# Loading the parameters of a mixer and making its tables during the feed-forward before it, in a four-layer decoder trunk

## The chip, the cores and the metric

The kernel runs on one core of one Trainium2 chip. The metric is the device time of one execution in microseconds (us); the time of a kernel is the median of several runs. Engines: PE is the matrix engine, with a queue of its own for loading weights (PEld), DVE the vector engine, ACT the scalar engine, POOL the general one, and SP the engine whose queue issues the DMAs.

## What is computed

Four layers over 256 tokens of width 1024, in float32. Each layer has three sub-layers, and each of those is applied as

```python
x = layer_norm(DN_ALPHA * x + f(x), g, b)
```

The first sub-layer is the mixer: a Conformer convolution in layers 0 and 3, a Mamba-2 mixer in layer 1, differential attention in layer 2. The second is attention to 256 memory tokens, the third a SwiGLU feed-forward. Of the mixers, what bears on the change is where small parameters enter:

```python
# Conformer: w_dw is 31 taps x 1024 channels
h = a * sigmoid(gate)                      # a, gate = split(x @ w_in + b_in)
h = causal_depthwise_conv(h, w_dw, b_dw)
# Mamba-2: 32 heads; w_conv 4 x 4096, b_conv 4096, norm_g 2048; dt_bias, a_log, d_skip 32 numbers each
dt = softplus(dt + dt_bias); a = -exp(a_log)
y = y + d_skip * xs
# differential attention: lam from exp(sum(lq1 * lk1)) - exp(sum(lq2 * lk2)); subln_g 128 numbers
```

## The kernel before

The 256 tokens are two tiles of 128. x stays on the chip; its transpose is kept as a sum of two reduced-precision parts, XTh and XTl, and every product of float32 matrices is three matmuls (`mm3`, L176 to L178: high x high, low x high, high x low). All weights are streamed, each once, in 537 blocks of 128 x 1024 numbers (512 KB). `_Weights` reads a plan of the whole order of blocks, which a first pass of the same program has recorded, and fetches three blocks ahead. For a block, SP issues a DMA into one of four buffers raw (L125), ACT casts it to wh (L132), and DVE subtracts in two halves to make the rest wl (L135); wh and wl have rings of seven buffers. The raw buffers also serve for other loads of up to 128 x 1024 numbers: the DFT constants (dft), the taps, the rows of the Mamba-2 parameters, some biases. A load that takes a raw buffer has to wait until the block that was in it has been cast and subtracted, and the blocks after it do with one buffer less until its own reader is done.

Each engine carries out its instructions in the order of the program as a scheduler has placed them, and a DMA on SP waits there, with all that is behind it, until its buffer is free. After each sub-layer `post_norm` adds and normalises x tile by tile (L311 the sum, L219 the statistics, L318 and L323 the norm, on DVE) and transposes it again on PE (L196; the splits are L183 on ACT and L185 on DVE). Between these, PE works on kv units, the projections of the memory for the next attention (psi from MTh, MTl).

The mixers begin with their small parameters, in the mixer's own code:

- `conv` (layers 0 and 3) multiplies by w_in in four pieces, `gated(0)` to `gated(3)`, and does the depthwise convolution through a real DFT over 160 points. After `gated(0)` it loads dft into a raw buffer (L465) and splits it, loads taps into another (L475) and the bias yre (L480), makes the spectra H of the taps by four float32 matmuls of 31 rows (L483; the chip records two for each), which ACT copies out of PSUM (L484), and, in layer 0, loads and transposes the memory (L364). Then come `gated(1)` and the rest.
- `ssd` (layer 1) loads sd_rows and sd_rows2 into two raw buffers (L712, L714, L715), transposes them on PE, loads sd_dcol by two DMAs of 64 x 16 single numbers (L727), sd_dtb (L732) and sd_ea (L734), and ACT takes the exponential of sd_ea (L735). Its first matmuls make dt.
- `diff` (layer 2) loads da_lv by four DMAs (L1044) and da_sg by one (L1056), multiplies and sums da_lv on DVE (L1047, L1050), takes an exponential on ACT (L1051), scales da_sg (L1057) and makes a mask.

`ff` works through 11 chunks of 256 hidden columns. All tile pools of a stage are opened with the default rule for their memory's reuse.

Of the kernel before, what the change touches and what calls it, by code (L numbers as in the profile page):

```python
# [9 lines left out]
F32 = mybir.dt.float32  # L10
# [7 lines left out]
P = 128  # L18
# [52 lines left out]
class _Trace:  # L71
    """Stands for the engines and the tiles while the order of the weight blocks is recorded."""
# [16 lines left out]

class _Weights:  # L90
    """Streams [128, nk, n] blocks of the weights and splits each into two float32r parts,
    whose sum is the float32 block."""
# [51 lines left out]
class _Trunk:  # L144
# [28 lines left out]
    def mm3(self, out, ah, al, bh, bl, start, stop):  # L173
        """Adds the float32 product of two split operands (a stationary, b moving)."""
# [5 lines left out]
    def split(self, src, dh, dl, scale=1.0):  # L180
        """dh + dl = scale * src, dh and dl in float32r."""
# [23 lines left out]
    def rstd(self, var, eps, cols, scale=1.0):  # L205
        """(scale * var + eps) ** -0.5"""
# [36 lines left out]
    def gemm_a(self, name, i, segs, done, which="o"):  # L243
        """x @ w[:, segs] for 512 columns, natural: tile 0 through all of them, then tile 1."""
# [15 lines left out]
    def out_mm(self, acc, t, h, w, first, last):  # L260
        """Adds rows h (128 of them, transposed) times their block of weights, tokens of tile t."""
# [16 lines left out]
    def out_tail(self, acc, name, i, ks, hs, ln, nxt=True, first=False):  # L278
        """The last blocks: tile 0 through all of them, then tile 1, each with its LayerNorm."""
# [15 lines left out]
    def new_xt(self, wanted=True):  # L295
        """The transposed activations for the next stage, if there is one."""
# [106 lines left out]
    def conv(self, i, j):  # L403
        """The depthwise convolution goes through a real DFT of 160 points over the tokens: tile t's
        128 outputs need the 30 tokens before them and its own."""
# [631 lines left out]
    def diff(self, i, j):  # L1037
# [3 lines left out]
        with tc.tile_pool(name="da", bufs=1) as pool, tc.tile_pool(name="dw", bufs=2) as wk:  # L1041
            lv = pool.tile([P, 4, 64], F32, name="da_lv")
            for q, name in enumerate(("da_lq1", "da_lk1", "da_lq2", "da_lk2")):
                nc.sync.dma_start(out=lv[:, q, :], in_=ins[name][j].partition_broadcast(P))  # L1044
# [275 lines left out]
```

## Time and profile before

| | us |
|---|---|
| runs (3), median and extremes | 1792.8 (1787.34 to 1801.01) |
| span of the profiled execution, first to last instruction | 1784.0 |
| PE busy | 1726.5 (97%) |
| DVE busy | 1241.6 (70%) |
| ACT busy | 850.0 (48%) |
| mean granted clock of PE | 0.987 |

The profiled execution's time outside its span is not recorded; the median of the runs is 8.8 us above the span, the fastest run 3.3 us. A row of the windows gives, for a stretch of time, the busy time of each engine with the number of its instructions, the clock granted to PE as a share of the full one, the busy share of the DMA engines and the rate. A row of a timeline gives start, duration, engine, line and operation, and in brackets how long the engine was idle before it and what ended that; SPq is SP issuing a DMA.

### The profile page before, as it was taken

The numbers are of one execution on the slowest core, as the hardware profiler recorded it, in microseconds if no ns is written. First come the engines' busy times: TensorE is split into PE (matmuls) and PEld (weight loads), VectorE is DVE, ScalarE is ACT, GpSimd is POOL, SyncE is SP. The second block draws the span as 40 slices with busy tenths as digits, with TensorE's granted clock in tenths as the row PEclk, the third lists the DMA queues.
The fourth block names the chain that finished last, engine by engine and source line by source line (L and its number), as shares of the span: only waits on it lengthen the run. The fifth ranks groups of instructions, "written<-read, shape, count | busy, mean of one in ns | idle before, by whom it ended". The sixth has DMA issues, their size and how long they took to land.

```text
span 1784.0 us, 29260 instructions
## 1 busy us (share of the span) xinstructions
PE 1726.5 (97%) x11356; PEld 1558.5 (87%) x11356; DVE 1241.6 (70%) x2296; ACT 850.0 (48%) x1258; POOL 56.2 (3%) x72
## 2 busy tenths in 40 slices
PE   7999999996999999999999999999999999999998
PEld 4887889996999998889998889889999688879997
DVE  4888675555898877685557677775556688775555
ACT  4445444442666654544444565544443445544442
POOL 0000000000010110000000000000000000000000
PEclk8999999998999999999999999999999899999999
DMA  6736365552866554465656643546555545646662
GB/s 215 225 116 224 130 210 181 189 189 64 248 175 198 160 164 159 151 195 184 191 186 182 191 135 124 177 154 212 180 188 165 184 146 177 189 153 190 189 188 72
DMA packets 235970, 310.00 MB, mean 174 GB/s; under 512 B 16038, under 2 KB 198646, under 8 KB 235832
## 3 DMA queue, kind: packets, MB, share of 16 engines
q1 hardware_dynamic: 235832, 308.14, 54.9%
q8 instruction: 89, 1.46, 0.3%
q14 instruction: 49, 0.40, 0.1%
HBM read 307.02 MB, written 1.08 MB: 173 GB/s over the span
## 4 chain that ended last, share of the span: by engine, by line
PE 73%; DVE 8%; DMA 5%; ACT 2%; issue 1%; SPq 1%; POOL 0%; DVEq 0%; ACTq 0%; POOLq 0%
PE psi L176 15%; PE psi L178 15%; PE psi L177 15%; PE pso L268 5%; PE pso L267 5%; PE pso L271 5%; DVE wl L135 3%; PE pso L176 2%; PE pso L178 2%; PE pso L177 2%; ACT wh L132 1%; DMA raw<-in_xa_w_q 1%; DVE st L219 1%; DVE x L311 1%; DVE x L323 1%
## 5 line engine op out<-in xcount | busy, mean ns | idle before, releaser
L135 DVE TENSOR_TENSOR wl<-raw,wh 128x512 fp32r<-128x512 f32 x1074 | 704.0, 685 | 418.7 <-ACT wh L132 415.9
L132 ACT CAST wh<-raw 128x1024 fp32r<-128x1024 f32 x537 | 560.4, 1049 | 670.8 <-PE psi L177 301.2
L176 PE MATMUL psi<-XTh,wh 128*128 128x256 f32 x1792 | 509.4, 284 | 0.2
L178 PE MATMUL psi<-XTh,wl 128*128 128x256 f32 x1792 | 507.2, 283 | 0.0
L177 PE MATMUL psi<-XTl,wh 128*128 128x256 f32 x1792 | 506.9, 283 | 0.0
L176 PEld LDWEIGHTS psi<-XTh,wh 128*128 128x128 f32 x1792 | 343.7, 192 | 2.9 <-issue 1.1
L177 PEld LDWEIGHTS psi<-XTl,wh 128*128 128x128 f32 x1792 | 343.7, 192 | 1.8
L178 PEld LDWEIGHTS psi<-XTh,wl 128*128 128x128 f32 x1792 | 343.7, 192 | 0.2 <-issue 0.2
L267 PE MATMUL pso<-wh,ch 128*128 128x512 f32 x448 | 176.1, 393 | 0.0
L268 PE MATMUL pso<-wl,ch 128*128 128x512 f32 x448 | 175.3, 391 | 0.0
L271 PE MATMUL pso<-wh,cl 128*128 128x512 f32 x448 | 139.3, 391 | 0.0
L271 PEld LDWEIGHTS pso<-wh,cl 128*128 128x128 f32 x448 | 84.0, 188 | 17.8
L268 PEld LDWEIGHTS pso<-wl,ch 128*128 128x128 f32 x448 | 84.3, 188 | 15.5
L267 PEld LDWEIGHTS pso<-wh,ch 128*128 128x128 f32 x448 | 84.4, 188 | 15.4 <-ACT ch L183 0.2
L176 PE MATMUL pso<-wh,XTh 128*128 128x512 f32 x224 | 89.5, 400 | 0.5 <-ACT XTh L183 0.4
L178 PE MATMUL pso<-wh,XTl 128*128 128x512 f32 x224 | 88.9, 397 | 0.3 <-DVE XTl L185 0.2
L177 PE MATMUL pso<-wl,XTh 128*128 128x512 f32 x224 | 87.6, 391 | 0.0
L176 PE MATMUL psi<-MTh,wh 128*128 128x256 f32 x256 | 73.6, 287 | 8.4 <-ACT wh L132 8.4
L211 POOL TENSOR_TENSOR rs<-rv,mhalf 128x1 f32<-128x1 f32 (+2 forms) x40 | 37.0, 926 | 1266.3 <-DVE rv L210 1254.0
L176 PE MATMUL pso<-wh,ch 128*128 128x512 f32 x192 | 75.9, 397 | 0.0
L178 PE MATMUL pso<-wh,cl 128*128 128x512 f32 x192 | 74.5, 392 | 0.0
L177 PE MATMUL pso<-wl,ch 128*128 128x512 f32 x192 | 74.5, 391 | 0.0
(294 smaller groups left out, 2660.2 us busy)
## 6 DMA issues: line engine op xcount, KB each, us to landing
raw<-in_ff_w_in SPq DMA_DIRECT2D x160, 512.0 KB, 3.5
raw<-in_ff_w_out SPq DMA_DIRECT2D x88, 512.0 KB, 3.3
raw<-in_xa_w_kv SPq DMA_DIRECT2D x64, 512.0 KB, 3.8
raw<-in_cv_w_in SPq DMA_DIRECT2D x64, 256.0 KB, 3.3
raw<-in_xa_w_q SPq DMA_DIRECT2D x32, 512.0 KB, 4.4
raw<-in_xa_w_out SPq DMA_DIRECT2D x32, 512.0 KB, 4.6
raw<-in_mb_w_in SPq DMA_DIRECT2D x32, 512.0 KB, 3.8
raw<-in_da_w_qkv SPq DMA_DIRECT2D x24, 512.0 KB, 4.4
```

Of the source, the lines that this page charges most:

```text
L132: nc.scalar.copy(out=wh, in_=raw)
L135: nc.vector.tensor_tensor(out=wl[:, a : a + m], in0=raw[:, a : a + m], in1=wh[:, a : a + m].bitcast(F32), op=ALU.subtract)
L176: mm(out, ah, bh, start=start, stop=False)
L177: mm(out, ah, bl, start=False, stop=False)
L178: mm(out, al, bh, start=False, stop=stop)
L211: nc.gpsimd.tensor_tensor(out=r, in0=v, in1=self.mhalf[:, :cols], op=ALU.pow)
L219: nc.vector.bn_stats(out=st[:, h, :], in_=halves[h])
L267: mm(acc[t][c], hh[:, ts], wh[:, 0, cs], start=first, stop=False)
L268: mm(acc[t][c], hh[:, ts], wl[:, 0, cs], start=False, stop=False)
L271: mm(acc[t][c], hl[:, ts], wh[:, 0, cs], start=False, stop=last)
L311: nc.vector.scalar_tensor_tensor(out=x[:, cs], in0=x[:, cs], scalar=self.alpha, in1=acc[t][c], op0=ALU.mult, op1=ALU.add)
L323: nc.vector.scalar_tensor_tensor(out=x[:, cs], in0=x[:, cs], scalar=r, in1=b[:, cs], op0=ALU.mult, op1=ALU.add)
```

## The change

The small parameters of a mixer are loaded, and the tables made from them, during the feed-forward of the layer before. `ff` gets hooks: at chunk 3 the loads, at chunk 5 the tables, at chunk 7 (for the convolution of layer 3) dft with its split and yre. The places where the instructions then stand follow from the scheduler. For layer 0 there is no feed-forward before; its ftap (the 31 x 164 part of dft that the taps need) and taps are loaded at the very beginning, into two raw buffers, the tables are made right after the set-up, and dft follows after `gated(0)`. The loads of ftap and taps are issued on ACT's queue in both convolutions. DVE instead of ACT copies H. sd_dcol is no longer loaded by single numbers: sd_dall holds all 32 numbers in each partition, and DVE copies every second one. All stage pools are opened with waits tile by tile. Beyond layer 0, ftap, taps and dft, and sd_rows and sd_rows2, have buffers in a pool of their own and take none of raw's.

```diff
+class _FromRaw:
+    def tile(self, shape, dtype, tag, name):
+        return self.raw.tile([P, D], dtype, tag="raw", name=name)[0 : shape[0], 0 : shape[1]]
...
+    def stage_pool(self, name, bufs):
+        return self.tc.tile_pool(name=name, bufs=bufs, reuse_waits="tile")
...
+    def conv_loads(self, pool, tmp, j):
+        ftap = tmp.tile([TAPS, 2 * NC], F32, tag="small", name=self.uid("ftap"))
+        nc.scalar.dma_start(out=ftap, in_=ins["dft"][0:TAPS, 4 * NC : 6 * NC])
+        taps = tmp.tile([TAPS, D], F32, tag="rows", name=self.uid("taps"))
+        nc.scalar.dma_start(out=taps, in_=ins["cv_w_dw"][j])
...
+    def conv_tables(self, pool, j, pre):
...
+                nc.tensor.matmul(ps[0:NC, :], ftap[:, q * NC : (q + 1) * NC], taps[:, cs], start=True, stop=True)
+                nc.vector.tensor_copy(out=pre["H"][q][:, cs], in_=ps[0:NF, :])
...
             gated(0)
-            dft = self.raw.tile([P, D], F32, tag="raw", name=self.uid("dft"))[:, 0:DFT_COLS]
-            nc.sync.dma_start(out=dft, in_=ins["dft"])
...
+            if "late" in pre:
+                pre.pop("late")()
...
-            taps = self.raw.tile([TAPS, D], F32, tag="raw", name=self.uid("taps"))
-            nc.sync.dma_start(out=taps, in_=ins["cv_w_dw"][j])
...
-                    nc.tensor.matmul(ps[0:NC, :], ftap[q], taps[:, cs], start=True, stop=True)
-                    nc.scalar.copy(out=H[q][:, cs], in_=ps[0:NF, :])
...
             for c in range(1, NFF):
+                for step in hooks.get(c, ()):
+                    step()
...
+    def ssd_loads(self, pool, tmp, j):
+        rows = tmp.tile([P, P], F32, tag="rows", name="sd_rows")
+        nc.sync.dma_start(out=rows, in_=ins["mb_w_conv"][j].rearrange("k (a b) -> (k a) b", b=P))
...
+        for n, src in (("dall", "mb_d"), ("dtb", "mb_dt_bias"), ("ea", "mb_a_log")):
+            pre[n] = pool.tile([P, 32], F32, name="sd_" + n)
+            nc.sync.dma_start(out=pre[n], in_=ins[src][j].partition_broadcast(P))
...
+        for q in range(2):
+            nc.vector.tensor_copy(out=dcol[64 * q : 64 * q + 64], in_=heads[64 * q : 64 * q + 64, :, q])
+        nc.scalar.activation(out=pre["ea"], in_=pre["ea"], func=AF.Exp)
...
-            for q in range(2):
-                nc.sync.dma_start(
-                    out=dcol[64 * q : 64 * q + 64],
-                    in_=ins["mb_d"][j].rearrange("(a b) -> a b", b=2)[:, q].partition_broadcast(64),
-                )
...
+        pre, (loads, tables, late) = self.prepare(0, ctx, _FromRaw(self.raw))
+        loads()
         self.setup()
+        tables()
+        pre["late"] = late
...
+                made["pool"] = tmp.enter_context(self.stage_pool(f"tmp{i + 1}", 1))
+                hooks = {3 + 2 * k: [step] for k, step in enumerate(steps)}
+            self.ff(i, i < DEPTH - 1, hooks)
```

In the changed kernel the helpers' lines are shifted: the weight DMA is L145, the cast L152, the subtraction L155, `mm3` L199 to L201, the spectra of the taps L444.

How the instructions move, at three places. A row has the line, the operation, what it writes and reads, and the size; a number in a name is that of the buffer's use (raw127 is the 128th block). First SP at the beginning of the Mamba-2 mixer, before:

```order
L125 DMA raw127_4290<-in_xa_w_kv 128x4x256
L125 DMA raw128_4321<-in_xa_w_kv 128x4x256
L712 DMA sd_rows_4364<-in_mb_w_conv 128x128
L727 DMA sd_dcol_4376<-in_mb_d 64x16x1 x2
L714 DMA sd_rows2_4366<-in_mb_b_conv 32x128
L715 DMA sd_rows2_4366<-in_mb_norm_g 16x128
L732 DMA sd_dtb_4379<-in_mb_dt_bias 128x32
L734 DMA sd_ea_4381<-in_mb_a_log 128x32
L125 DMA raw129_4384<-in_mb_w_in 128x4x256
L125 DMA raw130_4422<-in_mb_w_in 128x4x256
```

and where these loads stand on SP in the changed kernel, at the beginning of layer 0's feed-forward:

```order
L145 DMA raw59_2292<-in_ff_w_in 128x2x256 x2
L749 DMA sd_rows_2809<-in_mb_w_conv 128x128
L751 DMA sd_rows2_2811<-in_mb_b_conv 32x128
L145 DMA raw60_2300<-in_xa_w_kv 128x4x256
L752 DMA sd_rows2_2811<-in_mb_norm_g 16x128
L756 DMA sd_dall_2814<-in_mb_d 128x32
L756 DMA sd_dtb_2816<-in_mb_dt_bias 128x32
L756 DMA sd_ea_2818<-in_mb_a_log 128x32
L145 DMA raw61_2307<-in_xa_w_kv 128x4x256
```

All of them have moved by some 70 blocks, to both sides of raw60; at the mixer's beginning raw127 to raw132 now follow one another on SP. Second, ACT at the beginning of the Mamba-2 mixer, before:

```order
L132 CAST wh126_4175<-raw126_4172 128x1024
L183 ACTIVATE ch_301_4147<-fh2_300_4145 128x512
L735 ACTIVATE sd_ea_4381<-sd_ea_4381 128x32
L132 CAST wh127_4292<-raw127_4290 128x1024
L132 CAST wh128_4323<-raw128_4321 128x1024
```

and ACT at the beginning of layer 0's feed-forward, in the changed kernel:

```order
L152 CAST wh57_2155<-raw57_2152 128x1024
L152 CAST wh58_2163<-raw58_2160 128x1024
L780 ACTIVATE sd_ea_2818<-sd_ea_2818 128x32
L152 CAST wh59_2295<-raw59_2292 128x1024
L152 CAST wh60_2302<-raw60_2300 128x1024
```

The exponential of sd_ea stood ahead of the casts of wh127 and wh128 and now stands ahead of those of wh59 and wh60. Third, PE in `gated(0)` of the first convolution, in the changed kernel:

```order
L199 MATMUL psi_28_234<-wh1_189,XTh_3_98 128x512
L200 MATMUL psi_28_234<-wl1_190,XTh_3_98 128x512
L201 MATMUL psi_28_234<-wh1_189,XTl_4_99 128x512
L444 MATMUL psm_9_149<-taps_2_89,ftap_1_87 82x512
L444 MATMUL psm_10_152<-taps_2_89,ftap_1_87 82x512
L199 MATMUL psi_28_234<-wh2_197,XTh_3_98 128x512
L444 MATMUL psm_11_155<-taps_2_89,ftap_1_87 82x512
L444 MATMUL psm_12_158<-taps_2_89,ftap_1_87 82x512
L200 MATMUL psi_28_234<-wl2_198,XTh_3_98 128x512
```

Before, the four matmuls stood after the last of `gated(0)`'s, with dft and taps issued on SP behind raw6. Now they stand between those of wh1 and wh2. On SP, raw2 now waits until wl0 is made, raw3 for wl1, raw4 for wl2, raw5 for the fourth L444, and dft and mem come after raw6. In layer 2's feed-forward the other four L444 stand among the matmuls of that stage, not all in one piece.

More of the change, by code (lines that the diff above doesn't have):

```diff
@@ L87, in __exit__, with __init__, tile @@
         return False
+class _FromRaw:
+    def __init__(self, raw):
+        self.raw = raw
+    def tile(self, shape, dtype, tag, name):
+        return self.raw.tile([P, D], dtype, tag="raw", name=name)[0 : shape[0], 0 : shape[1]]
+class _Late:
+    def __init__(self, made):
+        self.made = made
+    def tile(self, *a, **k):
+        return self.made["pool"].tile(*a, **k)
 class _Weights:
@@ L463, in conv @@
             gated(0)
-            dft = self.raw.tile([P, D], F32, tag="raw", name=self.uid("dft"))[:, 0:DFT_COLS]
-            nc.sync.dma_start(out=dft, in_=ins["dft"])
-            dfts = [pool.tile([P, DFT_COLS], F32R, name="cv_dft" + e) for e in "hl"]
-            self.split(dft, *dfts)
+            if "late" in pre:
+                pre.pop("late")()
+            dfts, H, yre = pre["dft"], pre["H"], pre["yre"]
             now = [[d[:, q * NC : (q + 1) * NC] for d in dfts] for q in range(2)]
             past = [[d[:, (2 + q) * NC : (3 + q) * NC] for d in dfts] for q in range(2)]
-            ftap = [dft[0:TAPS, (4 + q) * NC : (5 + q) * NC] for q in range(2)]
             back = [[d[0 : NC - q, 6 * NC + q * P : 6 * NC + (q + 1) * P] for d in dfts] for q in range(2)]
@@ L542, in xattn @@
         ln = self.load_ln(i, 1)
[L543 removed]
+        with self.stage_pool(f"xa{i}", 2) as wk:
             def parts(n, tag, **k):
@@ new lines, in ssd_tables @@
+    def ssd_tables(self, pool, pre):
+        nc = self.nc
+        rows, rows2 = pre.pop("rows")
+        upper = pre["upper"] = pool.tile([P, P], F32, name="sd_upper")
+        nc.vector.memset(upper, 1.0)
+        nc.gpsimd.affine_select(
+            out=upper, in_=upper, pattern=[[1, P]], compare_op=ALU.is_ge, fill=0.0, base=0, channel_multiplier=-1
+        )
+        ones = pre["ones"] = pool.tile([P, P], F32, name="sd_ones")
+        nc.vector.memset(ones, 1.0)
+        ps = self.bank("m")
+        nc.tensor.transpose(ps[:, 0:P], rows, self.ident)
+        nc.tensor.transpose(ps[:, P : P + 48], rows2, self.ident[0:48, 0:48])
+        cw = pre["cw"] = pool.tile([P, 160], F32, name="sd_cw")
+        nc.vector.tensor_scalar(out=cw, in0=ps[:, 0:160], scalar1=0.5, scalar2=0.0, op0=ALU.mult, op1=ALU.add)
+        ng = pre["ng"] = pool.tile([P, 16], F32, name="sd_ng")
+        nc.vector.tensor_copy(out=ng, in_=ps[:, 160:176])
+        dcol = pre["dcol"] = pool.tile([P, 16], F32, name="sd_dcol")
+        heads = pre.pop("dall").rearrange("p (a b) -> p a b", b=2)
+        for q in range(2):
+            nc.vector.tensor_copy(out=dcol[64 * q : 64 * q + 64], in_=heads[64 * q : 64 * q + 64, :, q])
+        nc.scalar.activation(out=pre["ea"], in_=pre["ea"], func=AF.Exp)
@@ L701, in ssd @@
+    def ssd(self, i, j, pre):
         nc, ins = self.nc, self.ins
         tc = self.tc
[L703 to L735 removed]
@@ L739, in ssd @@
+        with self.stage_pool("sd", 1) as pool, self.stage_pool("sw", 1) as wk:
+            upper, ones, cw, ng, dcol, dtb, ea = (
+                pre[n] for n in ("upper", "ones", "cw", "ng", "dcol", "dtb", "ea")
+            )
             wh, wl = self.W.get("mb_w_in", j, 0, KT, (DT0, 32), (0, 96))
```

156 lines of the change are left out of this document (83 added, 73 removed).

## The prediction

> **What bounds the kernel now.** I read the page first, for the share of each engine and the chain that ended last.
>
> ```profile
> span 1784.0 us, 29260 instructions
> PE 1726.5 (97%) x11356; PEld 1558.5 (87%) x11356; DVE 1241.6 (70%) x2296; ACT 850.0 (48%) x1258; POOL 56.2 (3%) x72
> PE 73%; DVE 8%; DMA 5%; ACT 2%; issue 1%; SPq 1%; POOL 0%; DVEq 0%; ACTq 0%; POOLq 0%
> L135 DVE TENSOR_TENSOR wl<-raw,wh 128x512 fp32r<-128x512 f32 x1074 | 704.0, 685 | 418.7 <-ACT wh L132 415.9
> L132 ACT CAST wh<-raw 128x1024 fp32r<-128x1024 f32 x537 | 560.4, 1049 | 670.8 <-PE psi L177 301.2
> ```
>
> TensorE (PE) is busy for 97% of the span, so nothing that only spares DVE, ACT or the DMAs pays. The change can win only where PE stands still, or where it is busy at less than the full clock. 537 weight blocks in 1784 us are 3.3 us a block; that is the pace which the loads must keep. So I went to the windows at each place that the diff touches, then to the timelines of the engines in them. The columns are: stretch; its length; busy time and instructions of PE, weight load, DVE, ACT, POOL; granted clock; DMA share; GB/s. First the beginning of the Mamba-2 mixer:
>
> ```profile
> 428.00:432.00 4.00, 0.18 (x2) 0.00 (x0) 0.00 (x0) 0.00 (x0) 0.00 (x0) 0.83 0.05 0
> 432.00:436.00 4.00, 0.00 (x0) 0.00 (x0) 0.00 (x0) 0.60 (x2) 0.00 (x0) 0.50 0.12 19
> 436.00:440.00 4.00, 2.16 (x7) 1.65 (x7) 3.25 (x6) 2.97 (x5) 0.00 (x0) 0.50 0.00 0
> 440.00:444.00 4.00, 0.00 (x0) 0.00 (x0) 4.00 (x9) 0.00 (x0) 0.93 (x1) 0.50 0.47 136
> 444.00:448.00 4.00, 3.42 (x18) 3.45 (x19) 3.08 (x5) 3.13 (x4) 0.00 (x0) 0.54 0.95 299
> ```
>
> In these 20 us PE is busy for 0.18 + 2.16 + 3.42 = 5.76 us, nearly all at half clock, so it does about 0.2 + 5.6 / 2 = 3 us of full-speed work: **17 us are lost in this one pause**. Its cause stands in the timelines of SP's queue and of the three engines:
>
> ```profile
> 409.60 0.34 SPq L712 DMA_DIRECT2D sd_rows<-in_mb_w_conv  x1
> 412.79 1.43 SPq L727 DMA_DIRECT2D sd_dcol<-in_mb_d  x2
> 414.34 3.01 SPq L714 DMA_DIRECT2D sd_rows<-in_mb_b_conv  x1
> 417.40 6.83 SPq L715 DMA_DIRECT2D sd_rows<-in_mb_norm_g  x1
> 424.28 1.76 SPq L732 DMA_DIRECT2D sd_dtb<-in_mb_dt_bias  x1
> 426.09 0.43 SPq L734 DMA_DIRECT2D sd_ea<-in_mb_a_log  x1
> ...
> 435.40 0.23 ACT L735 ACTIVATE sd_ea<-sd_ea 128x32 f32<-128x32 f32 x1 [23.79 <-DMA sd_ea<-in_mb_a_log]
> ...
> 436.60 0.69 DVE L135 TENSOR_TENSOR wl<-raw,wh 128x512 fp32r<-128x512 f32 x1 [15.66 <-ACT wh L132]
> ...
> 436.62 0.58 PE L176 MATMUL psi<-MTh,wh 128*128 128x256 f32 x1 [8.44 <-ACT wh L132]
> 444.58 1.09 PE L196 MATMUL psm<-ident,x 128*128 128x128 f32 x4 [5.80 <-DVE x L323]
> ```
>
> Only the first two issues are quick; behind the two loads of sd_dcol (4-byte elements) every issue drags, and while SP takes 6.83 us over norm_g the DMA engines move next to nothing. The exponential of sd_ea waits 23.79 us on ACT. The casts of wh127 and wh128 are behind it in ACT's order, DVE waits 15.66 us for the cast, the second tile's norm and transposes are behind that on DVE, and PE waits twice (8.44 and 5.80 us).
>
> **The Mamba-2 loads (the main term).** The change takes all of this out of the mixer's beginning. The casts of wh127 and wh128 no longer have anything of the loads ahead of them, the two raw buffers that held sd_rows are free for weights, and the 4-byte loads are gone: sd_dall comes as rows of 32 numbers, like sd_dtb, and two DVE copies pick dcol out. What remains is a beginning like the others; the start of differential attention has the same order of work, and its worst window is
>
> ```profile
> 960.00:964.00 4.00, 3.21 (x21) 2.68 (x21) 4.00 (x8) 3.80 (x6) 0.05 (x1) 1.00 0.02 4
> 956.31 0.23 DVE L1047 TENSOR_TENSOR da_lv<-da_lv 128x64 f32<-128x64 f32 x1 [0.74 <-DMA da_lv<-in_da_lk]
> 958.69 0.23 DVE L1057 TENSOR_SCALAR da_sg<-da_sg 128x128 f32<-128x128 f32 x1 [0.19 <-DMA da_sg<-in_da_subln_g]
> ```
>
> that is, 0.8 us lost. 17 - 1 = **16 us gained**, bounds 13 (weights still late behind the quiet time) and 17.5. In their new place, the feed-forward of layer 0, the loads are six issues on SP around raw60, and the exponential stands ahead of the cast of wh59:
>
> ```profile
> 209.24 4.56 SPq L125 DMA_DIRECT2D raw<-in_xa_w_kv  x2
> 222.53 2.00 ACT L132 CAST wh<-raw 128x1024 fp32r<-128x1024 f32 x2 [7.79 <-PE pso L178]
> ```
>
> Between the two raw issues of that row SP has 4 us to spare, for four issues of 0.4 us. sd_ea is issued at about 211.5 and ACT needs it by 222.5: 11 us of cover, against the few us that a small load takes when nothing of 4 bytes is ahead of it (the da_lv and da_sg rows above made DVE wait 0.74 and 0.19 us only). Price here: nothing; without the cover it is the second rival. Two PE transposes and four small DVE instructions go with them, under half a microsecond of PE, which only changes place.
>
> **The first convolution's beginning.**
>
> ```profile
> 19.20 0.25 SPq L475 DMA_DIRECT2D taps<-in_cv_w_dw  x1
> 28.03 7.08 PE L483 MATMUL psm<-taps,dft 31*82 31x512 f32 x8 [3.83 <-DMA taps<-in_cv_w_dw]
> ...
> 24.00:28.00 4.00, 0.19 (x1) 0.00 (x1) 0.71 (x2) 0.00 (x0) 0.00 (x0) 0.98 0.90 259
> 28.00:32.00 4.00, 3.97 (x5) 1.35 (x6) 0.42 (x1) 1.16 (x3) 0.00 (x0) 0.50 0.22 88
> 32.00:36.00 4.00, 4.00 (x9) 1.46 (x7) 0.00 (x0) 1.48 (x3) 0.00 (x0) 0.50 0.00 0
> 36.00:40.00 4.00, 4.00 (x21) 3.38 (x21) 1.56 (x3) 1.93 (x4) 0.00 (x0) 0.74 0.85 259
> ...
> raw<-in_cv_w_in SPq DMA_DIRECT2D x24, 256.0 KB, 5.1
> mem<-in_mem SPq DMA_DIRECT2D x2, 512.0 KB, 8.4
> ```
>
> Lost here: 3.8 us of waiting for taps, then half the clock for 8 us and a quarter of it for 4 us more: 3.8 + 4 + 1 = 8.9 us. The eight records of L483 took 0.885 us each at half clock, so 0.44 us at full clock, 3.5 us together. That work is not removed: it goes between wh1's and wh2's matmuls, where PE runs at full clock. Against the gain stands that ftap and taps now hold two of the four raw buffers until the last of these matmuls. A buffer's round is then landing 5.1 + cast 1.05 + two subtractions 1.37 = 7.5 us; with two of them a block comes every 3.8 us, while PE uses one (12 matmuls; 17 take 4 us at a clock of 0.87, by the last row of the next fence) in 2.5. For about five blocks that is up to 1.3 us each, 6.5 us, partly filled by the 3.5 us of moved matmuls. dft, and after it mem, go out only when wl3 is made: raw3 is issued at about 13 us, when wl1 is done, so wl3 is there at 20.5, and mem0 lands near 30, just after gated(1) has begun. I take **5 us gained**; bounds: 9 (all of it), and a loss of 2 (full starvation, and the transposes of mem0 waiting 4 us).
>
> The trace has no load on ACT's queue. Bounds for the second queue: nothing, and 0.6 us, if 144 KB (taps, ftap) at 250 GB/s go ahead of x and raw0; I put it at 0.3, inside the 5. The Trainium skill, DMA: Bandwidth & Descriptors, section "Issuing engines are not separate DMA queues", says that a second issuing engine saves only issue time, since all transfers share the same 16 engines. By that page the upper bound of 0.6 holds and the sum below is 0.3 us smaller; no run here shows it yet.
>
> **The second convolution's beginning.**
>
> ```profile
> 1403.42 3.67 PE L483 MATMUL psm<-taps,dft 31*82 31x512 f32 x4 [2.49 <-DMA taps<-in_cv_w_dw]
> 1407.91 3.70 PE L483 MATMUL psm<-taps,dft 31*82 31x512 f32 x4 [0.81 <-ACT cv_H L484]
> ...
> 1400.00:1404.00 4.00, 1.51 (x6) 0.77 (x5) 0.00 (x0) 0.00 (x0) 0.00 (x0) 0.93 0.26 90
> 1404.00:1408.00 4.00, 3.19 (x5) 0.61 (x4) 2.10 (x4) 2.68 (x4) 0.00 (x0) 0.50 0.04 13
> 1408.00:1412.00 4.00, 4.00 (x5) 1.23 (x6) 1.33 (x3) 1.72 (x4) 0.00 (x0) 0.50 0.77 225
> 1412.00:1416.00 4.00, 4.00 (x11) 3.04 (x11) 2.22 (x4) 2.22 (x3) 0.00 (x0) 0.50 0.87 248
> 1416.00:1420.00 4.00, 4.00 (x17) 3.30 (x16) 1.72 (x3) 0.00 (x0) 0.00 (x0) 0.87 0.90 314
> ```
>
> Waiting 2.5 + 0.8, and half of 3.2 + 4 + 4 and an eighth of 4 for the clock: 3.3 + 5.6 + 0.5 = 9.4 us. Here all four raw buffers stay with the weights, since taps and dft get a pool of their own. The 3.5 us of matmuls go into the feed-forward of layer 2, where PE has no gap: neutral at full clock. What the trace leaves open is whether these matmuls, which use 31 of 128 rows, pull the clock down by themselves. In both places it stayed at 0.50 through all of L483 (28 to 36, and 1404 to 1412 us), though PE was busy, and came back only with full matmuls. If they do that in the feed-forward, they cost 3.5 us more there and slow the matmuls behind them as at 1412 to 1418 (2 + 0.5 us): 6 us, and 3.4 are left. Bounds 3.4 and 9.4; in the new order the four are not in one piece, so I take **6.5**. The Trainium skill, TensorE: Matmul & The Clock Gate, section "What's actually happening", has it that a busy window of some 3.4 us gives the full clock and an idle one takes it. By that page L444 in a busy feed-forward costs nothing, and the sum would be 3 us larger; the rows speak against it as far as L483's 7 us of unbroken work did not bring the clock back.
>
> **The rest.** Differential attention's start: da_sg's late arrival cost 0.2 to 0.8 us, so **1**, bounds 0 and 2. The tables' copies of H move from ACT to DVE (four of about 0.6 us; DVE is 70% busy): nothing, hidden behind PE. Pools that wait tile by tile take away waits that I find nowhere ahead of PE: nothing, at most 1. On ACT in layer 2's feed-forward, the issue of taps waits for raw350's landing, for which the cast behind it waits anyway: nothing. The dft load there stands on SP ahead of raw389 and waits for the last L444: hidden by the blocks already fetched ahead.
>
> **Sum.** 16 + 5 + 6.5 + 1 = 28.5 us: a span of 1755.5. The median of the runs is 8.8 us above the profiled span (1792.8 against 1784.0); with the same 8.8 the time is **1764 us**.
>
> **The rivals.**
> 1. The beginning starves: two raw buffers are too few, and the first convolution loses 2 instead of gaining 5. Sum 21.5, time 1771. For it: the 3.8 against 2.5 us a block; against it: PE has L444 to do meanwhile. 0.12.
> 2. The 31-row matmuls take the clock down wherever they stand: 2 and 3.4 us instead of 5 and 6.5. Sum 22.4, time 1770. For it: the clock rows; against: interleaving. 0.13.
> 3. sd_ea is late again. If the series of loads takes as long as it did (409.60 to 435.4, 25.8 us), sd_ea lands at about 235 in the feed-forward, 12 us after ACT needs it; with the slow clock afterwards 15 us. Sum 13.5, time 1779. Against it: the 4-byte loads are gone, and the dragging began with them. 0.08.
> 4. Slower than before: the pause belongs to small parameter loads on SP's queue, not to the 4-byte ones, and weights queued behind them stop. Then it comes whole, 17 us, in the feed-forwards of layers 0 and 1, and the gain there is spent: 28.5 - 34 = -5.5, time 1798. It decides from 14 us a place. For it: norm_g's issue, of ordinary 512-byte rows, took the longest (6.83 us); against it: five such loads at the start of differential attention made nobody wait a full microsecond. 0.05.
> That the change does not do what it says is excluded by the order of the instructions.
>
> **How the numbers follow.** The forecast has 0.62. A measurement of this kernel tells about 1% (18 us) from no change, so faster means below 1775. The forecast is nearly all below that (0.60), rivals 1 and 2 mostly (0.17), the third seldom (0.01): 0.78. Slower than 1811 takes a worse case of the fourth: 0.04. The rest, 0.18, is the same. Lower bounds of the gains together (13 - 2 + 3.4 + 0 = 14.4) give 1778, the upper ones (17.5 + 9 + 9.4 + 2 = 38) 1755; with about 5 us for the scatter of medians the range is 1750 to 1783, and it leaves out the fourth rival.
>
> **What would show it.** Right: between 425 and 445 us no PE wait over 3 us and a clock of 1.0; no wait of ACT for sd_ea over 1 us near 215; gated(1) of the first convolution begins near 30 us, where before L483 alone lasted until 35.1; no slow clock where the second convolution begins. Wrong: a DMA share near zero for over 10 us in a feed-forward, ACT waiting there for sd_ea, raw waits of ACT in the first 50 us that exceed those of before by more than 5 us, or a clock of 0.5 where L444 now stands.

## The result and the profile after

The median of the changed kernel is 1763.1 us (1761.0 to 1766.6, four runs) against 1790.1 us (1785.1 to 1801.0, four runs) on the same chip: a ratio of 0.985, 95% interval 0.982 to 0.987. The prediction said 1764 and 1750 to 1783. The profiled span is 1760.3 us; the prediction's sum gave 1755.5. From the page of the changed kernel, the span and the engines:

```profile
span 1760.3 us, 29243 instructions
PE 1718.8 (98%) x11356; PEld 1555.8 (88%) x11356; DVE 1247.9 (71%) x2306; ACT 844.6 (48%) x1250; POOL 55.6 (3%) x72
```

PE does the same 11356 matmuls in a span that is 23.7 us shorter. Where these came from is read from one small DVE instruction, the variance of each norm (L210 before, L233 after), which marks the end of a stage. In a convolution the mark taken is that of the norm inside it, behind the depthwise part; "the convolution's end" below is this mark. Its start in the two traces, in us:

| mark | before | after | gained so far |
|---|---|---|---|
| norm inside the first convolution (its end, below) | 117.13 | 118.04 | -0.9 |
| Mamba-2 mixer begins, first tile | 417.54 | 417.31 | 0.2 |
| the same, second tile | 442.31 | 426.09 | 16.2 |
| end of the mixer | 694.30 | 677.73 | 16.6 |
| differential attention begins, second tile | 967.60 | 951.06 | 16.5 |
| its end | 1113.25 | 1096.99 | 16.3 |
| layer 2's feed-forward begins | 1183.01 | 1165.69 | 17.3 |
| the same feed-forward's end | 1378.46 | 1366.90 | 11.6 |
| norm inside the second convolution (its end, below) | 1474.21 | 1449.75 | 24.5 |
| last norm | 1778.32 | 1754.50 | 23.8 |

The norms at the very end of the two convolution sub-layers come at 152.29 and 152.14 us, and at 1511.67 and 1487.56: 0.2 and 24.1 gained so far. The gain comes in two places and is partly given back in a third. Differences of some 5 us or less are not read from the marks of two traces alone: two kernels here that issue the same instructions up to the mixer (the kernel before and the first experiment below) stand 2.6 us apart at the first convolution's end and 5.4 us apart at 418 us.

**The mixer's beginning** has no pause any more. The windows of the changed kernel there (the same columns as in the prediction):

```profile
424.00:428.00 4.00, 4.00 (x35) 4.00 (x35) 4.00 (x9) 0.01 (x1) 0.92 (x1) 1.00 0.57 149
428.00:432.00 4.00, 4.00 (x36) 4.00 (x35) 4.00 (x8) 3.56 (x5) 0.00 (x0) 1.00 1.05 307
436.00:440.00 4.00, 4.00 (x36) 4.00 (x35) 3.21 (x8) 2.69 (x5) 0.00 (x0) 1.00 0.95 305
```

PE is busy for the whole 4 us of each of these windows at the full clock (from 444 to 448 us it is idle for 1.6 us), and the DMA engines, which moved almost nothing there before, run at 300 GB/s from 428 us on. In the place where the loads now stand, ACT's timeline shows the wait for sd_ea and the cast behind it:

```profile
216.38 0.23 ACT L780 ACTIVATE sd_ea<-sd_ea 128x32 f32<-128x32 f32 x1 [1.37 <-DMA sd_ea<-in_mb_a_log]
222.80 2.00 ACT L152 CAST wh<-raw 128x1024 fp32r<-128x1024 f32 x2 [6.19 <-PE pso L201]
```

ACT waits 1.37 us for it, and the next cast is due 6 us later and waits for PE, not for ACT: the cover held.

**The second convolution** begins without a gap, and the clock stays up:

```profile
1380.00:1385.00 5.00, 5.00 (x24) 4.12 (x23) 4.37 (x8) 1.54 (x2) 0.00 (x0) 1.00 0.97 297
1395.00:1400.00 5.00, 5.00 (x24) 4.14 (x23) 3.94 (x6) 2.47 (x4) 0.00 (x0) 1.00 0.93 298
```

By the marks it gained 24.46 - 11.56 = 12.9 us, which is 9.4 of waits and slow clock and 3.5 of matmuls that moved away. Layer 2's feed-forward, where these matmuls now stand, lost 5.8 (201.21 us between the marks against 195.45). Its PE timeline and windows, in the changed kernel:

```profile
1257.21 2.94 PE L444 MATMUL psm<-taps,ftap 31*82 31x512 f32 x6
1260.75 1.08 PE L444 MATMUL psm<-taps,ftap 31*82 31x512 f32 x2
```
```profile
1256.00:1260.00 4.00, 4.00 (x12) 1.46 (x10) 2.69 (x5) 1.04 (x1) 0.00 (x0) 1.00 0.77 254
1260.00:1264.00 4.00, 4.00 (x17) 2.99 (x17) 2.16 (x4) 0.00 (x0) 0.00 (x0) 0.71 0.28 65
1264.00:1268.00 4.00, 4.00 (x31) 4.00 (x30) 1.07 (x2) 1.77 (x2) 0.00 (x0) 0.86 0.42 167
```

The records take 2.94 / 6 = 0.49 us each, near the 0.44 of the full clock; but from 1260 us on the clock falls to 0.71 and 0.86, though PE is never idle. That costs 4 x 0.29 + 4 x 0.14 = 1.7 us, with the matmuls themselves (3.6 to 3.9 us) 5.3 to 5.6 of the 5.8.

**The first convolution** gained nothing. Its part of the waits of PE up to 118 us in the changed kernel, and rows of PE's timeline:

```profile
PE psm L219 <- DMA x<-in_x: 7.0, 2, 4.8
PE psi L199 <- ACT XTh L206: 4.9, 1, 4.9
...
PE psi L200 <- DVE wl L155: 0.5, 2, 0.2
```
```profile
14.07 0.80 PE L199 MATMUL psi<-wh,XTh 128*128 128x512 f32 x1 [4.86 <-ACT XTh L206]
...
21.17 1.94 PE L444 MATMUL psm<-taps,ftap 31*82 31x512 f32 x4 [0.35 <-DVE XTl L208]
```

The 3.8 us of waiting for taps are gone, and the wait for weights is 0.5 us; but the very first matmul with weights starts at 14.07 us. In the kernel before it was:

```profile
8.95 0.79 PE L176 MATMUL psi<-wh,XTh 128*128 128x512 f32 x1 [2.79 <-ACT XTh L183]
```

So 5.1 us are lost before any product with weights has been made. What releases that matmul is the copy XTh on ACT, which stands behind the cast of the first weight block there, and ACT's timeline says why that cast is late (before, it started at 7.36 us):

```profile
12.47 1.04 ACT L152 CAST wh<-raw 128x1024 fp32r<-128x1024 f32 x1 [9.40 <-DMA raw<-in_cv_w_in]
```

The clock takes a second part. In the windows behind the eight L444 of this stage, and again behind a wait of 2.5 us at 64 us, it falls:

```profile
24.00:28.00 4.00, 4.00 (x12) 2.36 (x11) 3.23 (x6) 2.09 (x2) 0.00 (x0) 0.76 0.89 308
28.00:32.00 4.00, 4.00 (x16) 3.23 (x15) 1.66 (x3) 1.29 (x2) 0.00 (x0) 0.81 0.94 298
...
64.00:68.00 4.00, 2.42 (x11) 2.00 (x12) 3.73 (x8) 2.06 (x3) 0.00 (x0) 0.88 0.64 218
68.00:72.00 4.00, 4.00 (x19) 3.36 (x18) 3.25 (x6) 1.58 (x2) 0.00 (x0) 0.69 0.42 133
```

That is 4 x 0.24 + 4 x 0.19 = 1.7 us for the first pair and as much for the second; in the kernel before, a wait of 2.1 us at the same place left the clock at 1.00. Late start and clock together take 8.5 us, nearly as much as the 8.9 of waiting and slow clock that are gone from this stage.

### The profile page after: what moved, and what is told of

Read it like the earlier page. It is cut to its first block, busy times and chain, and to the rows that moved or that the text cites. A ratio compares the mean times of both kernels' runs of the same rounds, so it can differ in the third digit from the quotient of the medians.

```text
span 1760.3 us, 29243 instructions
## 1 busy us (share of the span) xinstructions
PE 1718.8 (98%) x11356; PEld 1555.8 (88%) x11356; DVE 1247.9 (71%) x2306; ACT 844.6 (48%) x1250; POOL 55.6 (3%) x72
## 3 DMA queue, kind: packets, MB, share of 16 engines
HBM read 307.07 MB, written 1.08 MB: 175 GB/s over the span
## 4 chain that ended last, share of the span: by engine, by line
PE 72%; DVE 9%; DMA 5%; ACT 2%; issue 2%; SPq 0%; POOL 0%; DVEq 0%; ACTq 0%; POOLq 0%
PE psi L199 14%; PE psi L200 14%; PE psi L201 14%; PE pso L291 5%; PE pso L290 5%; PE pso L294 5%; DVE wl L155 3%; PE pso L199 2%; PE pso L201 2%; PE pso L200 2%; DMA raw<-in_xa_w_q 2%; ACT wh L152 1%; DVE st L242 1%; DVE x L334 1%; DVE x L346 1%
## 5 line engine op out<-in xcount | busy, mean ns | idle before, releaser
L155 DVE TENSOR_TENSOR wl<-raw,wh 128x512 fp32r<-128x512 f32 x1074 | 704.3, 686 | 396.8 <-ACT wh L152 394.5
L152 ACT CAST wh<-raw 128x1024 fp32r<-128x1024 f32 x537 | 560.3, 1048 | 686.6 <-PE psi L200 312.9
L199 PE MATMUL psi<-XTh,wh 128*128 128x256 f32 x1792 | 510.4, 285 | 0.2
L201 PE MATMUL psi<-XTh,wl 128*128 128x256 f32 x1792 | 507.7, 283 | 0.0
L199 PEld LDWEIGHTS psi<-XTh,wh 128*128 128x128 f32 x1792 | 344.4, 192 | 3.9 <-issue 2.0
L201 PEld LDWEIGHTS psi<-XTh,wl 128*128 128x128 f32 x1792 | 344.4, 192 | 0.0
L199 PE MATMUL pso<-wh,XTh 128*128 128x512 f32 x224 | 89.5, 400 | 0.5 <-ACT XTh L206 0.4
L201 PE MATMUL pso<-wh,XTl 128*128 128x512 f32 x224 | 88.9, 397 | 0.3 <-DVE XTl L208 0.2
L199 PE MATMUL pso<-wh,ch 128*128 128x512 f32 x192 | 76.0, 397 | 0.0
L201 PE MATMUL pso<-wh,cl 128*128 128x512 f32 x192 | 74.6, 392 | 0.0
L199 PE MATMUL psi<-wh,MTh 128*128 128x256 f32 x256 | 73.6, 287 | 0.5 <-DVE memVl L208 0.4
```

The lines of the kernel that those rows point to most:

```text
L152: nc.scalar.copy(out=wh, in_=raw)
L155: nc.vector.tensor_tensor(out=wl[:, a : a + m], in0=raw[:, a : a + m], in1=wh[:, a : a + m].bitcast(F32), op=ALU.subtract)
L199: mm(out, ah, bh, start=start, stop=False)
L201: mm(out, al, bh, start=False, stop=stop)
```

## The experiments

The first theory, from these rows: the two loads on ACT's queue, of 31 rows each, run through very few DMA engines and hold up x and the first weight blocks; the mixer's gain belongs to the form of sd_dcol's load; and the 31-row matmuls lower the clock by themselves. The rivals were that the second queue itself is the disturbance, that two raw buffers starve the beginning, that moving the loads and not their form is what counts, and that the clock answers to PE's idle time alone. Each ratio below is to the kernel before on the same chip.

**1. The form of sd_dcol's load alone.** The kernel before, its loads left where they were, with sd_dall and two copies in place of the two 4-byte loads:

```
-  nc.sync.dma_start(out=dcol[64*q:64*q+64], in_=ins["mb_d"][j].rearrange("(a b) -> a b", b=2)[:, q]...)
...
+  nc.sync.dma_start(out=dall, in_=ins["mb_d"][j].partition_broadcast(P))
...
+  nc.vector.tensor_copy(out=dcol[64*q:64*q+64], in_=heads[64*q:64*q+64, :, q])
```

> The kernel before with one edit: sd_dcol comes from sd_dall, a load of whole rows, and two DVE copies; all loads stay at the mixer's beginning. Theory: the pause belongs to the two loads of 4-byte elements; 12 to 15 of its 16 us go by this edit alone, ACT waits for sd_ea less than 4 us, the time is 1775 to 1778 (1790 before). Rival: the pause belongs to the place, small loads ahead of the weights at a mixer's start whatever their form; at most 5 us go, the time stays above 1784.

Measured: 1771.1 us (1768.4 to 1777.8), ratio 0.990 [0.988, 0.992]. The two tiles' norms at the mixer's beginning stand 8.78 us apart, as in the changed kernel; in the kernel before it was 24.77. The totals of the DMA view from 412 to 432 us, first of the kernel before, then of this one:

```profile
DMA packets 1901, 0.02 MB, mean 1 GB/s; under 512 B 1900, under 2 KB 1900, under 8 KB 1900
```
```profile
DMA packets 1300, 0.80 MB, mean 40 GB/s; under 512 B 500, under 2 KB 1298, under 8 KB 1298
```

Before, 20 us were filled with 1900 packets that carry 0.02 MB in all. Here the small ones are 500, and SP's and ACT's timelines and the windows read:

```profile
418.07 0.34 SPq L727 DMA_DIRECT2D sd_dall<-in_mb_d  x1
...
419.87 0.41 SPq L734 DMA_DIRECT2D sd_ea<-in_mb_a_log  x1
```
```profile
423.76 0.23 ACT L735 ACTIVATE sd_ea<-sd_ea 128x32 f32<-128x32 f32 x1 [6.87 <-DMA sd_ea<-in_mb_a_log]
```
```profile
428.00:432.00 4.00, 4.00 (x35) 4.00 (x35) 4.00 (x10) 0.00 (x0) 0.00 (x0) 1.00 0.16 25
432.00:436.00 4.00, 4.00 (x36) 4.00 (x35) 3.33 (x6) 2.11 (x4) 0.93 (x1) 1.00 0.99 315
```

Every issue takes 0.4 us again. ACT's wait is longer than was expected (6.87; sd_ea is issued at 419.87 and there at 423.76), and still PE is busy throughout these windows; from 416 to 448 us it is idle for no more than 1 us, nearly all at 440 to 444, so this wait costs next to nothing. The whole pause goes with the form of the load; the place is not needed for it.

**2. The place alone.** The changed kernel, with the two 4-byte loads kept and moved along with the others into layer 0's feed-forward:

```
+  for q in range(2):
+      nc.sync.dma_start(out=dcol[64*q:64*q+64], in_=ins["mb_d"][j].rearrange("(a b) -> a b", b=2)[:, q]...)
...
-  for n, src in (("dall", "mb_d"), ("dtb", "mb_dt_bias"), ("ea", "mb_a_log")):
+  for n, src in (("dtb", "mb_dt_bias"), ("ea", "mb_a_log")):
```

> The change with one edit: sd_dcol is again loaded by two DMAs of 4-byte elements, now in the feed-forward of layer 0. Theory: the same trickle of DMAs then stands in the feed-forward; ACT waits for sd_ea there 15 us or more instead of 1.4, the feed-forward is 8 to 15 us longer, the time 1771 to 1778. Rival: in the feed-forward it is hidden, and the time is that of the change (1763).

Measured: 1774.5 us (1770.8 to 1777.1), ratio 0.992 [0.990, 0.994]. SP, ACT and the windows of this kernel in the feed-forward:

```profile
211.28 4.74 SPq L762 DMA_DIRECT2D sd_dtb<-in_mb_dt_bias  x1
...
218.53 23.49 SPq L145 DMA_DIRECT2D raw<-in_ff_w_in  x3
```
```profile
234.59 0.23 ACT L782 ACTIVATE sd_ea<-sd_ea 128x32 f32<-128x32 f32 x1 [20.25 <-DMA sd_ea<-in_mb_a_log]
```
```profile
228.00:232.00 4.00, 0.00 (x0) 0.00 (x0) 0.00 (x0) 0.00 (x0) 0.00 (x0) 0.72 0.38 67
232.00:236.00 4.00, 0.00 (x0) 0.00 (x0) 0.21 (x1) 1.41 (x3) 0.00 (x0) 0.50 0.50 170
```

The pause has moved: the two tiles' norms at the beginning of that feed-forward are 21.08 us apart instead of 8.77, so 12.3 us. This is the prediction's third rival, at 234.6 us where it had put 235. Work that is taken out of the path still costs most of its price in the new place (12.3 us of 16.0 here) if its cover (the 11 us of the prediction) is shorter than its delay (25 us from the first 4-byte issue at 209.81 to 234.59).

**3. The 31-row loads in two pieces.** The changed kernel, ftap and taps each loaded as 16 rows and 15 rows, still on ACT's queue:

```
-  nc.scalar.dma_start(out=taps, in_=ins["cv_w_dw"][j])
+  for a, b in ((0, 16), (16, TAPS)):
+      nc.scalar.dma_start(out=taps[a:b], in_=ins["cv_w_dw"][j][a:b])
...
```

> ftap and taps are each loaded by two DMAs of 16 and 15 rows instead of one of 31; nothing else changes. Theory A (a DMA of 31 rows goes through one DMA engine only, and x, raw0 and the load that waits behind it queue up there): the DMAs of the first 12 us no longer thin out to 26 GB/s, the first gated matmul begins at 9 to 10.5 us instead of 14.1, and the first convolution ends 4 to 5 us earlier: 1758.5 us. Rival B (two raw buffers held by ftap and taps starve the weights) and rival C (the second queue itself delays the first loads): the first matmul stays near 14 us, the time at 1763.

Measured: 1757.5 us (1752.7 to 1761.6), ratio 0.981 [0.979, 0.983], span 1754.8. The interval overlaps a little with that of the change (0.982 to 0.987), so the rows have to decide. The first convolution ends at 113.55 us: 3.6 gained. PE's first weight matmul in this kernel:

```profile
9.22 0.80 PE L199 MATMUL psi<-wh,XTh 128*128 128x512 f32 x1 [3.18 <-ACT XTh L206]
```

and the rates of the DMA view from 0 to 16 us, in 40 slices of 0.4 us, first of the changed kernel, then of this one:

```profile
GB/s 0 0 0 0 46 180 208 346 351 265 351 292 256 259 277 343 371 333 287 241 156 74 31 26 26 26 26 23 23 28 20 26 133 307 343 382 164 38 10 26
```
```profile
GB/s 0 0 0 0 41 167 128 373 331 264 309 323 328 248 179 330 346 366 379 371 348 369 341 356 284 74 18 15 225 264 228 305 243 195 120 115 100 205 302 379
```

From 8.8 to 12.8 us the changed kernel moves 20 to 31 GB/s, and from 9.2 to 12.5 us PE, ACT and DVE stand still: one trickle is left, in which taps and the last parts of SP's loads go by. By the trace's semaphores taps land at 11.75 us, with a single update behind the one at the issue, while the two halves of the first weight block have 15 of their 16 updates by 5.3 and 7.3 us and the last one at 11.5 and 12.4. SP's next weight issue waits 6.0 us for taps too (issued at 11.76 us in the changed kernel, at 6.28 here). So one engine of the sixteen has taps and a sixteenth of everything else, and whatever has a part on it is late. In pieces, the taps land within 5 us and the trickle is gone. The Trainium skill, DMA: Bandwidth & Descriptors, section "Why a DMA increments its semaphore by 16 and not by 1", gives the rule behind it: a transfer is spread over the largest number of engines up to 16 that divides its slowest dimension, so one engine for 31 rows, 16 for 16, 15 for 15. The single update and the rates agree.

**4. The other queue.** The changed kernel with the two loads of layer 0 first on SP's queue, in one piece each:

```
...
-  nc.scalar.dma_start(out=taps, in_=ins["cv_w_dw"][j])
+  (nc.scalar if j else nc.sync).dma_start(out=taps, in_=ins["cv_w_dw"][j])
```

> In layer 0 ftap and taps are issued on SP's queue, first of all, instead of ACT's; each is still one DMA of 31 rows. Theory A: no better than the change, first matmul between 13 and 15 us, since the rows still go through one engine. Rival C (the second queue is what delays): first matmul back at 9 to 10 us.

Measured: 1767.7 us, one run, span 1765.9. PE's timeline:

```profile
10.96 1.94 PE L219 MATMUL psm<-ident,x 128*128 128x128 f32 x8 [10.96 <-DMA x<-in_x]
14.59 0.80 PE L199 MATMUL psi<-wh,XTh 128*128 128x512 f32 x1 [1.69 <-ACT XTh L206]
```

The first weight matmul is as late (14.59) as from ACT's queue, so the second queue is not the cause, and with x behind them the loads hold up even the transposes. The Trainium skill, same page, section "Issuing engines are not separate DMA queues", says the transfers share the engines whoever issues them; this agrees.

**5 and 6. Layer 0's loads and tables late**, behind `gated(0)`, as in the kernel before; the rest as in the change. Once on ACT's queue, once on SP's (with the line of experiment 4):

```
-  loads()
   self.setup()
-  tables()
-  pre["late"] = late
+  pre["late"] = lambda: (late(), loads(), tables())
```

> The loads of ftap and taps and the tables of layer 0 go back behind gated(0), after dft; all else as in the change. If the beginning as changed brings nothing in sum (as the two traces say: its end is 0.9 us later than before), this is as fast as the change within 2 us, with the first gated matmul at 9 us again and the wait for taps back at about 24 us. If the early tables do bring the 5 us of the prediction somewhere, it is 4 to 6 us slower than the change.

> As the run with the tables of layer 0 behind gated(0) again, but ftap and taps go on SP's queue there instead of ACT's. Theory: a load of 31 rows goes through one DMA engine; on ACT's queue it shares that engine with what SP has issued, and landed 13 us after its issue; on SP's own queue it stands ahead of mem in that engine, as before, and lands about 9 us after its issue, so the first matmul of L444 begins near 28 to 30 us instead of 34. Rival: the later landing came from the order (ftap ahead of taps, and biases ahead of both), and it stays at 33 to 35.

Measured: 1769.1 us (1768.0 to 1775.8), ratio 0.989 [0.986, 0.991], from ACT's queue; 1762.0 us, one run, from SP's. PE in the first and in the second:

```profile
34.10 3.67 PE L444 MATMUL psm<-taps,ftap 31*82 31x512 f32 x4 [8.37 <-issue]
```
```profile
28.87 5.20 PE L444 MATMUL psm<-taps,ftap 31*82 31x512 f32 x6 [3.68 <-issue]
```

("issue" is here the wait for taps, for which the view names no releaser.) From ACT's queue, taps land 13.4 us after their issue at 20.66, from SP's 8.3 us after 20.55, and PE stands still for 8.4 and 3.7 us. My expectation for the first, as fast as the change, missed by 6 us; the second gave what was asked: without the early load and tables of layer 0 the kernel is about as fast as the change (1762.0, a single run, against 1763.1, and 1760.2 for the change on the same chip), so that part of the change brought at most some 2 us as it was written.

**7. Rows of zeros in layer 2.** The changed kernel, with L444 in layer 2's feed-forward working on 128 rows: ftap with 128 rows, taps cleared and 31 rows loaded; the products are the same:

```
+  pad = P if j else TAPS
+  taps = tmp.tile([pad, D], F32, tag="rows", name=self.uid("taps"))
+  if j:
+      nc.gpsimd.memset(taps, 0.0)
...
```

> The change with one edit in layer 2's feed-forward: the four matmuls of L444 run over 128 rows instead of 31, the added rows being zeros (ftap's are zero in the DFT constants, those of taps are set on POOL first); same number of columns and same result. Theory: matmuls over 31 rows count as little activity, and the granted clock falls after them for that reason; with 128 rows it stays at 1.0 around them and the feed-forward of layer 2 is 1.5 to 2 us shorter. Rival: the clock falls for another reason (float32 matmuls, or waits between them), and stays at 0.7 to 0.9 in the windows behind L444 as in the change.

Measured: 1760.7 us, one run, span 1759.0. The feed-forward takes 199.23 us between the marks of the table against 201.21, 2.0 less. PE and the windows:

```profile
1258.55 2.89 PE L447 MATMUL psm<-taps,ftap 128*82 128x512 f32 x6
```
```profile
1260.00:1264.00 4.00, 4.00 (x22) 2.61 (x21) 3.45 (x6) 0.00 (x0) 0.00 (x0) 1.00 0.41 130
1264.00:1268.00 4.00, 4.00 (x36) 4.00 (x34) 1.80 (x3) 1.77 (x2) 0.00 (x0) 1.00 0.61 220
```

As many matmuls, as long (2.89 against 2.94 us for six), and the clock stays at 1.00 where it was 0.71 and 0.86. So the fall is due to the 31 rows and not to a gap. The other traces bear this out, with one exception. Of the eight with 31 rows in this feed-forward (the change twice, experiments 2 to 6 and 11) seven show the fall: the first slow window begins within 5 us of the first L444, the lowest is between 0.50 and 0.74, PE is busy throughout, and the feed-forward takes 200.9 to 203.3 us. In the eighth, that of experiment 2, the clock stays at 1.00 (199.96 us). In none of the four with 128 rows (experiments 7 to 10) does it fall, and they take 199.1 to 199.3 us. The 31 rows make the fall likely, not certain, and in some executions it lasts longer: in the change run again the windows from 1256 us on read 0.93, 0.50 and 0.72, which is 3.4 us.

**8 and 9. Both: pieces and zeros in layer 2**, run twice:

> The version that the runs point to: ftap and taps by DMAs of 16 and 15 rows in both convolutions, and in layer 2's feed-forward the matmuls of L444 over 128 rows, 97 of them zeros. If the two effects are independent, it gains 5 us of the first and 2 of the second over the change: 1756 us, granted clock 1.0 around L444 in layer 2's feed-forward, first gated matmul at 9 to 10 us. If the clock's fall at L444 in the feed-forward is only shifted to another place, the second part is missing and it is as fast as the split alone, 1757.5.

> The kernel with both splits and zeros in layer 2 alone, run again on the same chip as the one with zeros in both layers, for the comparison and for a second look at its beginning. Theory A (31-row matmuls hold the clock down): half speed for some us somewhere between 14 and 30 us again, how long depending on whether full speed was reached before the first of them; median 1755 within 3. Theory B: this beginning may come out clean (full speed from about 14 us on through all eight).

Measured: 1755.1 us (1748.8 to 1760.6), ratio 0.980 [0.978, 0.982], and 1751.8 us (1751.4 to 1757.1), ratio 0.980 [0.978, 0.982]: the lowest medians of the study, 35 to 37 us under the kernel before, though the intervals overlap with that of the pieces alone. The two profiled executions have the same program and end the first convolution 7.2 us apart, at 119.15 and 111.96. PE's timelines, in this order:

```profile
15.27 1.99 PE L449 MATMUL psm<-taps,ftap 31*82 31x512 f32 x2
...
19.20 3.70 PE L449 MATMUL psm<-taps,ftap 31*82 31x512 f32 x4
...
29.05 0.63 PE L201 MATMUL psi<-wh,XTl 128*128 128x512 f32 x1
```
```profile
14.96 1.08 PE L449 MATMUL psm<-taps,ftap 31*82 31x512 f32 x2
...
16.77 0.40 PE L200 MATMUL psi<-wl,XTh 128*128 128x512 f32 x1
17.09 1.94 PE L449 MATMUL psm<-taps,ftap 31*82 31x512 f32 x4
```

In the second, full speed had come by the first L449 (1.08 us for two records against 1.99), and nearly everything after it is fast. In the first it had not, and half speed (0.63) lasted until 29.05 us, some 20 us after the first matmul with weights; in the kernel before, in experiment 9 and in experiment 10 below full speed came 4 to 6 us after it. That the 31-row matmuls kept it away fits experiment 7, but it is read from these executions and not tested by itself. The windows print a clock of 1.00 in that stretch; at the very beginning the durations decide, not that column.

**10. Zeros in both layers.** The same kernel with 128 rows in layer 0 too (`n = P`):

> In this kernel the loads of ftap and taps are split in 16 rows and the rest, and L444's matmuls (here L448 or near) use 128 rows, 31 and 97 rows of zeros of taps, in layer 0 as well as in layer 2; the output is unchanged. It differs from the kernel with both splits and zeros in layer 2 alone only at the beginning. In that kernel's trace the first matmuls ran at half speed until 29.5 us (0.63 us records instead of 0.39 from 10.1 to 29.05), with eight 31-row matmuls of 0.92 to 1.0 us each among them; in the kernel before, without such matmuls there, full speed came at 14.4 us. Theory A: matmuls over 31 rows do not open the clock, and the half speed there is theirs. Then full speed comes by 16 us, the eight records take 0.5 to 0.6 us each, no window from 16 to 32 us is below 0.95, and the first convolution's end (the norm's variance) comes at 113 us or earlier, against 119.15; median 2 to 6 us below the other kernel of this call. Theory B: the clock opens at a moment that has nothing to do with the rows (a free-running window that was unlucky in that execution). Then half speed or a clock below 0.9 is seen somewhere between 16 and 32 us here too, or the two medians agree within 1.5 us. Price that could spoil it: the zeros are written first, so the loads of taps start about 1 us later, and ftap brings 84 KB instead of 20: below 1 us if the second weight block is not held up.

Measured: 1762.2 us (1759.4 to 1764.2), ratio 0.985 [0.984, 0.987]. Slower by 10 us than its neighbour, where 2 to 6 us faster was expected. PE and ACT:

```profile
13.20 0.80 PE L199 MATMUL psi<-wh,XTh 128*128 128x512 f32 x1 [6.98 <-ACT XTh L206]
...
18.16 1.88 PE L448 MATMUL psm<-taps,ftap 128*82 128x512 f32 x4
```
```profile
11.60 1.04 ACT L152 CAST wh<-raw 128x1024 fp32r<-128x1024 f32 x1 [2.48 <-DMA raw<-in_cv_w_in]
12.55 1.08 ACT L206 ACTIVATE XTh<-psm 128x512 fp32r<-128x512 f32 x2
```

The clock did what the theory said: eight records of 0.47 us at full speed, and a clock of 1.00 from 16 to 60 us; as experiment 9 has a clean beginning with 31 rows too, one trace does not prove it. But the order changed with the edit. The zeros stand on POOL ahead of the identity for the transposes, and on ACT the cast of wh1 now stands ahead of the first XTh, so the first matmul waits for the second weight block: 13.20 us instead of 9.35, and 4.5 us at the first convolution's end (116.44). Further 3.3 us went in layer 0's feed-forward, where one matmul waits 2.0 us for DVE. So the price of the 31 rows in layer 0 is not measured by this kernel's time, only by its rows.

**11. Pools that wait as a whole**, the changed kernel with the default rule for its stage pools (`reuse_waits="tile"` left out), and **12. the changed kernel again:**

> The stage pools are opened with the default rule again, all else as in the change. Theory: waits tile by tile bring nothing, the time is that of the change within 1 us (1763). Rival: they are what lets the loads of a mixer start inside the feed-forward; without them the moved loads wait for the stage before, and 3 us or more are lost in the feed-forwards.

> The changed kernel itself once more, unaltered, beside the run above on the same chip: 1763 us, first gated matmul at 14 us.

Measured: 1763.07 us (1759.7 to 1765.0), ratio 0.984 [0.982, 0.985], beside the change's 1763.05; and 1760.2 us (1759.4 to 1761.8), ratio 0.984 [0.982, 0.985], for the change itself. The rule for the pools made no difference that can be measured.

## Why the prediction was right, and the step of it that failed

The time and its sign were right, but the hit to 1 us is partly luck: the span was 4.8 us longer than the sum, and an error of the other sign in the step from span to median made up for it.

- **The mixer, 16 us.** Measured 16.0 between the two tiles' norms. The cause was named rightly as the 4-byte loads; experiments 1 and 2 show that it is their form and not their place. The moving as such had no part in this gain.
- **The second convolution, 6.5 us.** Measured 12.9 less 5.8, so 7.1. The open question there, whether 31-row matmuls lower the clock by themselves, is answered by experiment 7 and the traces beside it: mostly yes. The slow clock where L444 now stands, which the prediction had named as a sign of being wrong, did come. The second rival had the mechanism but too high a price: in this trace the matmuls themselves still ran at the full clock, since the fall comes some 4 us after the first of them, and only 1.7 us were lost behind them (3.4 us in the change run again, none in experiment 2).
- **The first convolution, 5 us: this is the step that failed.** Measured -0.9 (0.2 at the sub-layer's own norm and at 417 us; -0.3 in the change run again). The waiting for taps and the slow clock behind it, 8.9 us, were indeed gone. What was subtracted, 4 us for two raw buffers, hardly came (0.5 us of PE waiting for wl). In its place came what the prediction had put at 0.3 and at most 0.6: "144 KB (taps, ftap) at 250 GB/s". The bytes were right and the rate was not. At the trickle's 26 GB/s they take 5.5 us, and the late start measured 5.1. The rest went to the clock: 1.7 us behind L444, the second rival's mechanism, which the 5 had left out here, and 1.7 us behind the wait at 64 us. Of these parts the late start is shown by experiments 3 and 4 and comes again in every kernel with the loads in one piece at the beginning (13.9 to 14.6 us); the falls of the clock are read from one trace, and the change run again has only the second. With the loads in pieces the first convolution ended 3.6 and 5.2 us earlier than before in experiments 3 and 9, near the forecast of 5, but 2.0 us later in experiment 8, where half speed lasted.
- **Differential attention, 1 us.** -0.3 at its end; too small to tell.
- **Nothing for the pools, the copies of H on DVE and the small loads**: as measured, in experiment 11 and in the cover of sd_ea.
- **From the span to the median, 8.8 us.** This was too much: the changed kernel's median lies 2.75 us above its profiled span. Time and span of one run differ by 1.7 to 1.8 us (1762.06 and 1760.3); the rest was the scatter of the executions before (1785.1 to 1801.0), of which the profiled one happened to be short. The missing 4.8 us of the sum and these 6 us too many made the hit of 1 us; the sum of the terms is what should be judged.

Of the rivals, the first (starvation) had the right place and the wrong mechanism; the second is real at a lower price; the third came true in experiment 2 and was averted in the change by the form of the load; the fourth, small loads of any kind stopping the queue, is refuted by experiment 1.

**Open.** Whether two raw buffers in layer 0 cost anything by themselves was not tried. What the 31 rows cost in layer 0 varies with the moment at which full speed comes, from little to about 7 us (experiments 8 and 9), and no kernel here removed them with the order left alone.

## What to carry to other kernels

Look at the shape of a transfer before its bytes: a small parameter load can set the pace, be it by elements of 4 bytes or by a row count such as 31 that few engines share, and the remedy is its form (a contiguous row and a copy, or 16 rows and the rest), not its place. Work moved out of a stage must be priced in the new place with everything that it does to the clock and to the queues there. An edit that changes what a scheduler sees moves other instructions too, so read the order again before a time is put down to the edit.

## What the runs showed of the hardware

- The granted clock does not ask only whether PE is busy. Eight matmuls over 31 rows, with PE never idle, were followed by windows of 0.71 and 0.86, from some 4 us after the first of them on, and by such a fall in seven of eight traces; the same matmuls over 128 rows left it at 1.00 in all four. At the beginning, half speed lasted from 15 to 29 us among them in one of two executions of the same kernel. The Trainium skill, TensorE: Matmul & The Clock Gate, section "What's actually happening", has the default throttled and a busy window of about 3.4 us releasing it; a delay of that size agrees with these rows, but "busy" is not enough by them.
- While one transfer of 31 rows (124 KB) was under way, all that moved in the end was 20 to 31 GB/s, and what was issued with it on the other queue had its last sixteenth at about the time when it ended (11.5 and 12.4 us against 11.75). From ACT's queue, in the midst of SP's weight loads, the same load took 13.4 us to land, from SP's 8.3.
